# Delta rule products in turn between column halves, both directions in step, and the HGRN output's attention product with all 128 rows

## The chip, the cores and the metric

One core of one Trainium2 chip runs the whole program. The metric is the device time of one execution in microseconds. The engines are PE (matmuls), DVE (vector), ACT (activations), POOL and SP; SP issues most of the transfers.

## What is computed

One layer of a trunk over 2048 latent and 256 context tokens, width 1024. Four token mixers (HGRN2, gated DeltaNet, Fourier, Mamba-2 SSD) are merged by sigmoid gates, and a mixture of experts follows. Two of the mixers matter here. Both work on 4 heads of 64 channels, in chunks of 64 tokens, in a forward and a backward direction whose outputs are added:

```python
# gated DeltaNet, one direction: t_mat = I + strictly lower (beta k k^T L); u, w solve t_mat
def step(S, inp):
    u_c, w_c, qk_c, qd_c, kd_c, gl_c = inp
    v_new = u_c - w_c @ S
    o_c = qd_c @ S + qk_c @ v_new
    S = jnp.exp(gl_c)[..., None, None] * S + jnp.einsum("bhjd,bhje->bhde", kd_c, v_new)
    return S, o_c
# HGRN2, one direction
o = att @ vc + (qc * jnp.exp(g)) @ S
```

The gates are `sigmoid(h @ w_gate[g] + b_gate[g])`, four projections of 1024 x 1024 for all latent tokens.

## The kernel before

The program is written with a tile framework. The methods are called one after the other (`front`): projections, masks and decays, `gdn_heads` and `gdn_invert` (delta rule: matrices per head, inverses of 32x32 blocks), then `gdn_merge`, `gdn_chain`, `hgrn`, `ssd`, `fourier` and `gates`. When the kernel is built, the framework lays the instructions of each engine in one fixed order, with the order of the program text as priority and durations that it estimates, and adds the semaphores. So instructions of `gates` (its matmuls are lines 114 to 116 with the tiles `whi`, `wlo`, `h2h`, `h3h` and so on), though last in the text, stand between those of the mixers on PE wherever the planner saw room.

- `gdn_merge` (L1164 on) runs six rounds: two pairs of heads `b` times three groups of six token blocks. A round loads the inverted blocks D, R, F, B, and `pairs` (L1198) makes 64x64 products of them on PE (L1206): `Ao` with D, the result with R (it fills the open quarter of F and B), then the decayed keys `K` with F and with B (the W products). `i` is the head in the pair, `a` the half of the 128-token block. Each call of `pairs` makes four groups of six products; the group lies in one row half and one column half of the array, and ACT empties its PSUM tile (64 partitions). D and R use row half `a` and column half `a`; the W products use row half `a` and column half 64 to 127. F, B and W go to DRAM as `gLW`.
- `gdn_chain` (L1235 on) runs 36 steps over the chunks for each direction `d`. The tile `gX` holds 64 rows of values U and 64 rows of state S, for four heads. A step loads `gLt` (from `gLW`), makes four products of it with `gX` (L1266, K = 128 rows, output in partitions 0 to 63), multiplies by beta on DVE (L1267), decays S (L1273), makes four products of the keys `gKt` (64 rows) with U (L1278, output in partitions 64 to 127), adds them to S on DVE (L1279), and, for latent chunks, makes the output with `gAt` (L1287), whose four products write the lower and the upper 64 partitions in turn. The two directions follow each other within a step, each with its own PSUM tiles.
- `hgrn` (L826 on) works head by head. At its end each of 32 chunks gets two products that are summed in PSUM: L926, attention times values, takes 64 rows (`o` is the chunk's half of the tiles `hatt` and `hv`), and L928, state times queries, takes 128 rows. `hv` has zeros in the other half of the rows: they are written once, since L906 uses the tile with all rows. The output partitions are the half `r` that belongs to the head.

Of the kernel before, what the change touches and what calls it, by code (L numbers as in the profile page):

```python
# [18 lines left out]
D = 1024  # L19
# [26 lines left out]
class Kernel:  # L46
# [773 lines left out]
    def hgrn(self, p):  # L820
# [17 lines left out]
        for h in range(H):  # L838
# [80 lines left out]
            for g in range(2):  # L919
                for a in range(2):  # L920
                    ps = self.two()
                    o = 64 * a
# [100 lines left out]
    def gdn_heads(self, p):  # L1023
# [16 lines left out]
        for b in range(2):  # L1040
            for g in range(0, self.NP, G):
# [59 lines left out]
                for d, mk in ((0, "ge"), (1, "le")):  # L1101
                    ro = (d * nl + l0 // 64) * 32768
                    T = tl("gA", 4)
                    nc.vector.tensor_mul(T[:, ml:], Z[:, ml:], bc(self.tm[mk])[:, ml:])
                    for a in range(2):
                        nc.sync.dma_start(ap(rec, ro + a * 32768 + 128 * b, [[256, 64], [65536, nq], [1, 128]]),
                                          T[64 * a:64 * a + 64, ml:].rearrange("p m h i -> p m (h i)"))

                    gq = p.tile([128, n], F32, name="gE", bufs=2)
                    for i in range(2):  # L1110
                        r = slice(64 * i, 64 * i + 64)
                        self.bc_time(gq[:, 128 * ml:], 8 + 4 * d + 2 * b + i, CTX + l0, 128 * nq, r, 64)
                    nc.vector.tensor_mul(gq[:, 128 * ml:], gq[:, 128 * ml:], qT[:, 128 * ml:])
                    for i in range(2):
                        r = slice(64 * i, 64 * i + 64)
                        nc.sync.dma_start(ap(rec, ro + 64 * 256 + 64 * (2 * b + i), [[256, 64], [32768, 2 * nq], [1, 64]]),
                                          gq[r, 128 * ml:].rearrange("p (c i) -> p c i", i=64))
# [50 lines left out]
    def gdn_merge(self, p):  # L1168
# [10 lines left out]
        for b in range(2):  # L1179
            for g in range(0, NP, G):  # L1180
# [27 lines left out]

                def ev_q(ps, c, a, i):
                    nc.scalar.activation(Q[c, :, i], ps[c], AF.Copy)  # L1210
                pairs(Ao, blk["D"], ev_q)

                def ev_x(ps, c, a, i):
                    r0 = slice(64 * a, 64 * a + 32)
                    r1 = slice(64 * a + 32, 64 * a + 64)
                    nc.scalar.activation(blk["F"][r0, :, i, 32:], ps[r0, :, 32:], AF.Copy, scale=-1.0)
                    nc.scalar.activation(blk["B"][r1, :, i, :32], ps[r1, :, :32], AF.Copy, scale=-1.0)
                pairs(Q, blk["R"], ev_x)
                for d, n in ((0, "F"), (1, "B")):
                    K = p.tile(B4, F32, name="gK4", bufs=1)  # L1220
# [3 lines left out]
                    Wt = p.tile([128, G, 2, 2, 64], F32, name="gW4", bufs=1)  # L1224

                    def ev_w(ps, c, a, i):
                        nc.scalar.activation(Wt[c, :, a, i], ps[c], AF.Copy, scale=-1.0)
                    pairs(K, blk[n], ev_w, 64)
                    ro = (d * 36 + 2 * g) * 32768 + 128 * b
                    for a in range(2):  # L1230
                        nc.sync.dma_start(ap(gL, ro + a * 32768, [[256, 64], [65536, G], [1, 128]]),
                                          blk[n][64 * a:64 * a + 64].rearrange("p m h i -> p m (h i)"))
                    nc.sync.dma_start(ap(gL, ro + 64 * 256, [[256, 64], [32768, 2 * G], [1, 128]]),
                                      Wt[64:].rearrange("p m a h i -> p (m a) (h i)"))

    def gdn_chain(self, p, fp):
        nc = self.nc
        nl, ncx = SEQ // 64, CTX // 64
        gL, rec = self.dram("gLW", (2, 36, 128, 256)), self.dram("gAT", (2, nl, 128, 256))
        kh, gV = self.dram("gKH", (2, 36, 64, 256)), self.dram("gV", (TOT, W))  # L1240
        bU = p.tile([64, self.NT, 2, 8], F32, name="gbU")
        for a in range(2):
            nc.vector.tensor_copy(bU[:, :, a], self.beta[64 * a:64 * a + 64])
        oG = p.tile([128, 2, SEQ], F32, name="goT")
        order = [list(range(36)), list(range(ncx))[::-1] + list(range(ncx, 36))[::-1]]

        def newX(d, c):
            x = p.tile([128, 4, 64], F32, name=f"gX{d}", bufs=3)
            nc.sync.dma_start(x[:64], ap(gV, c * 64 * W, [[W, 64], [64, 4], [1, 64]]))
            return x  # L1250
        X = []
        for d in range(2):
            x = newX(d, order[d][0])
            nc.vector.memset(x[64:], 0.0)
            X.append(x)
        seen = set()
        for s in range(36):
            for d in range(2):
                c = order[d][s]
                x = X[d]  # L1260
                last = s == 35
                lw = p.tile([128, 4, 64], F32, name=f"gLt{d}", bufs=2)
                nc.sync.dma_start(lw, ap(gL, (d * 36 + c) * 32768, [[256, 128], [64, 4], [1, 64]]))
                ps = self.mx()
                for h in range(H):
                    nc.tensor.matmul(ps[:64, h * 64:h * 64 + 64], lw[:, h], x[:, h], start=True, stop=True)  # L1266
                nc.vector.tensor_tensor(x[:64], ps[:64, :256].rearrange("p (h e) -> p h e", e=64),  # L1267
                                        bU[:, c // 2, c % 2, 4 * d:4 * d + 4][:, :, None].to_broadcast([64, 4, 64]), op=OP.mult)
                if not last:
                    kt = p.tile([64, 4, 64], F32, name=f"gKt{d}", bufs=2)  # L1270
                    nc.sync.dma_start(kt, ap(kh, (d * 36 + c) * 16384, [[256, 64], [64, 4], [1, 64]]))
                    xn = newX(d, order[d][s + 1])
                    nc.vector.tensor_tensor(xn[64:], x[64:],  # L1273
                                            self.gl64[64:, c % 2, c // 2, 4 * d:4 * d + 4][:, :, None].to_broadcast([64, 4, 64]),
                                            op=OP.mult)
                    ps = self.mx()
                    for h in range(H):
                        nc.tensor.matmul(ps[64:, h * 64:h * 64 + 64], kt[:, h], x[:64, h], start=True, stop=True)  # L1278
                    nc.vector.tensor_tensor(xn[64:], xn[64:], ps[64:, :256].rearrange("p (h e) -> p h e", e=64), op=OP.add)  # L1279
                    X[d] = xn  # L1280
                if c >= ncx:
                    n = c - ncx
                    at = p.tile([128, 4, 64], F32, name=f"gAt{d}", bufs=2)
                    nc.sync.dma_start(at, ap(rec, (d * nl + n) * 32768, [[256, 128], [64, 4], [1, 64]]))
                    ps = self.mx()
                    for h in range(H):
                        nc.tensor.matmul(ps[64 * (h % 2):64 * (h % 2) + 64, h // 2 * 64:h // 2 * 64 + 64], x[:, h],  # L1287
                                         at[:, h], start=True, stop=True)
                    o = oG[:, :, n * 64:n * 64 + 64]
                    pv = ps[:, :128].rearrange("p (b i) -> p b i", i=64)  # L1290
# [964 lines left out]
```

## Time and profile before

| what | value |
|---|---|
| median of 3 runs | 3985.44 us (3971.31 to 3986.7) |
| the profiled execution | 3978.21 us, its span 3976.4 us |
| mean granted TensorE clock | 0.937 of 2.4 GHz |
| busy: PE, DVE, ACT, POOL | 3668.2, 2457.5, 1277.1, 904.1 us |

The span runs from the first to the last instruction. [...] Busy time of PE counts modelled ends of pipelined matmuls.

### The profile page before, as it was taken

The page shows a single profiled execution, that of the slowest core. Times are in us where ns is not written, and L with a number is a line of the kernel's source. Part 1 is how long each engine was busy: PE and PEld are TensorE (multiplying, and loading weights), DVE is VectorE, ACT ScalarE, POOL GpSimd, SP SyncE. Part 2 cuts the span into 40 slices and gives each one's busy share as a digit, 9 for nine tenths or more (in the row PEclk, how much of TensorE's full clock was granted, in tenths as well). Part 3 has the DMA queues.
Part 4 walks back from the last instruction along what each step waited for, and adds up shares of the span by engine and source line. Part 5 has one row for each costly group of instructions (what it writes and reads, how often), then busy time and mean ns, then how long its engine had stood idle before and what let it go on. Part 6 is the DMA issues. An engine that isn't in the chain of part 4 may idle for free. (4 is left out here: it accounts for less than half of the span.)

```text
span 3976.4 us, 60130 instructions
## 1 busy us (share of the span) xinstructions
PE 3668.2 (92%) x23407; PEld 3052.9 (77%) x23407; DVE 2457.5 (62%) x4454; ACT 1277.1 (32%) x1950; POOL 904.1 (23%) x636
## 2 busy tenths in 40 slices
PE   6999999998899999899889989994899999999997
PEld 3887778787777676667767767773799999999886
DVE  7538752275626477373875577788565555555887
ACT  3422232122425122142224322212334444444443
POOL 2000013311212110122341246564010000101243
PEclk9999999998969899897899999996899999999998
DMA  7534448756435456423356766643475665766875
GB/s 244 191 112 137 125 112 197 185 136 156 121 88 129 137 155 196 135 81 100 94 145 207 233 215 189 199 143 136 146 221 182 216 223 193 226 208 208 284 264 182
DMA packets 596812, 680.93 MB, mean 171 GB/s; under 512 B 152656, under 2 KB 469552, under 8 KB 593328
## 3 DMA queue, kind: packets, MB, share of 16 engines
q1 hardware_dynamic: 537136, 537.08, 44.2%
q0 software_dynamic: 24800, 90.71, 8.4%
q10 hardware_dynamic: 34592, 49.29, 3.6%
q8 instruction: 185, 3.03, 0.3%
q14 instruction: 99, 0.81, 0.1%
HBM read 514.88 MB, written 162.06 MB: 170 GB/s over the span
## 5 line engine op out<-in xcount | busy, mean ns | idle before, releaser
L107 POOL TENSOR_TENSOR wlo<-wraw,whi 128x1024 fp32r<-128x1024 f32 x60 | 147.5, 2458 | 687.9 <-ACT whi L105 622.8
L114 PE MATMUL big<-h2h,whi 128*128 128x512 f32 x704 | 295.3, 419 | 3.9 <-ACT ev L1566 3.9
L114 PE MATMUL mx<-exh,wgateh 128*128 128x256 f32 x1024 | 296.0, 289 | 0.0
L116 PE MATMUL big<-h2h,wlo 128*128 128x512 f32 x704 | 295.5, 420 | 0.5 <-DVE wlo L107 0.5
L115 PE MATMUL big<-h2l,whi 128*128 128x512 f32 x704 | 295.2, 419 | 0.0
L115 PE MATMUL mx<-exl,wgateh 128*128 128x256 f32 x1024 | 290.7, 284 | 0.0
L116 PE MATMUL mx<-exh,wgatel 128*128 128x256 f32 x1024 | 290.5, 284 | 0.0
L116 PE MATMUL big<-h3h,wlo 128*128 128x512 f32 x704 | 290.2, 412 | 0.0
L114 PE MATMUL big<-h3h,whi 128*128 128x512 f32 x704 | 289.9, 412 | 0.0
L115 PE MATMUL big<-h3l,whi 128*128 128x512 f32 x704 | 289.9, 412 | 0.0
L115 PE MATMUL mx<-exl,wuph 128*128 128x256 f32 x1024 | 289.8, 283 | 0.0
L116 PE MATMUL mx<-exh,wupl 128*128 128x256 f32 x1024 | 289.8, 283 | 0.0
L114 PE MATMUL mx<-exh,wuph 128*128 128x256 f32 x1024 | 289.8, 283 | 0.0
L2077 POOL DMA_INDIRECT d_acc<-ey,ix x30 | 50.7, 1690 | 780.2 <-DVE ey L2070 741.1
L116 PE MATMUL big<-wdh,hidl 128*128 128x512 f32 x496 | 196.4, 396 | 10.9 <-DVE hidl L107 10.9
L107 DVE TENSOR_TENSOR wdl<-wdr,wdh 128x1024 fp32r<-128x1024 f32 x124 | 153.7, 1240 | 81.5 <-ACT wdh L105 81.4
L115 PEld LDWEIGHTS mx<-exl,wgateh 128*128 128x128 f32 x1024 | 197.3, 193 | 2.8 <-DVE exl L107 0.3
L114 PEld LDWEIGHTS mx<-exh,wgateh 128*128 128x128 f32 x1024 | 197.3, 193 | 2.5
L107 DVE TENSOR_TENSOR wgatel<-wgr,wgateh 128x2048 fp32r<-128x2048 f32 x62 | 151.0, 2436 | 76.2 <-ACT wgateh L105 76.1
L2031 ACT ACTIVATE sg<-mx 128x256 f32<-128x256 f32 x128 | 49.1, 383 | 462.5 <-PE mx L116 462.5
L2032 DVE TENSOR_TENSOR sg<-sg,mx 128x256 f32<-128x256 f32 x128 | 53.7, 420 | 231.9 <-ACT sg L2031 231.8
L116 PEld LDWEIGHTS mx<-exh,wgatel 128*128 128x128 f32 x1024 | 196.8, 192 | 0.0
(641 smaller groups left out, 9875.3 us busy)
## 6 DMA issues: line engine op xcount, KB each, us to landing
wgr<-in_w_ff_gate_dram SPq DMA_DIRECT2D x64, 1024.0 KB
wgr<-in_w_ff_up_dram SPq DMA_DIRECT2D x64, 1024.0 KB
wdr<-in_w_ff_down_dram SPq DMA_DIRECT2D x128, 512.0 KB
wraw<-in_w_gate_dram POOLq DMA_DIRECT2D x64, 512.0 KB, 5.0
d_th<-ev ACTq DMA_DIRECT2D x128, 256.0 KB
bt<-d_th SPq DMA_DIRECT2D x128, 256.0 KB
adr<-in_ada_w_dram SPq DMA_DIRECT2D x128, 128.0 KB
bw<-in_w_branch_dram SPq DMA_DIRECT2D x64, 256.0 KB
```

The lines of the kernel that those rows point to most:

```text
L107: return (eng or self.nc.vector).tensor_tensor(lo, src, hi, op=OP.subtract)
L114: self.nc.tensor.matmul(ps, wh, xh, start=first and k == 0, stop=False)
L115: self.nc.tensor.matmul(ps, wh, xl, start=False, stop=False)
L116: self.at_pe = self.nc.tensor.matmul(ps, wl, xh, start=False, stop=last and k == n - 1).ins
L2031: silu.append(nc.scalar.activation(sg, ps[:, :CAP], AF.Silu).ins)
L2032: self.at_dve = nc.vector.tensor_mul(sg, sg, ps[:, CAP:]).ins
L2077: nc.gpsimd.indirect_dma_start(out=acc, out_offset=bass.IndirectOffsetOnAxis(ap=ix[e][:, k:k + 1], axis=0), in_=weighted(e, k), in_offset= ...
```

## The change

- HGRN output: L926 takes all 128 rows of `hv` and `hatt` in place of 64.
- Merge: in a group the products of the two halves `a` (D and R) or of the two directions (W) follow each other in turn, with one PSUM tile of 128 partitions for both; ACT empties 128 partitions at once. The keys of both directions are made first, in two tiles (`gK40`, `gK41`).
- Chain: direction 0 keeps U in partitions 0 to 63 and S in 64 to 127, direction 1 has them swapped. In a step the products of both directions stand in one group, head by head, direction by direction, in one PSUM tile; the DVE work follows for one direction and then the other. The output products come after both.
- The addresses of the blocks stored for direction 1 (`gLW`, `gAT`) are swapped to fit.

```diff
-    nc.tensor.matmul(out, v[o:o + 64, CTX // 128 + c // 2, a], att[o:o + 64, c // 2, :],
-                     start=True, stop=False)
+    nc.tensor.matmul(out, v[:, CTX // 128 + c // 2, a], att[:, c // 2, :], start=True, stop=False)
...
-    def pairs(lhs, rhs, evac, col=None):
-        for i in range(2):
-            for a in range(2):
-                ps = self.mx()
-                r = slice(64 * a, 64 * a + 64)
-                c = r if col is None else slice(col, col + 64)
-                for m in range(G):
-                    nc.tensor.matmul(ps[c, m * 64:m * 64 + 64], lhs[r, m, i], rhs[r, m, i], start=True, stop=True)
-                evac(ps[:, :64 * G].rearrange("p (m i) -> p m i", i=64), c, a, i)
+    def pairs(i, lhs, rhs):
+        ps = self.mx()
+        for m in range(G):
+            for a in range(2):
+                r = slice(64 * a, 64 * a + 64)
+                nc.tensor.matmul(ps[r, m * 64:m * 64 + 64], lhs[r, m, i], rhs[r, m, i], start=True, stop=True)
+        return ps[:, :64 * G].rearrange("p (m i) -> p m i", i=64)
+    for i in range(2):
+        nc.scalar.activation(Q[:, :, i], pairs(i, Ao, blk["D"]), AF.Copy)
...
+    rows = [slice(64, 128), slice(0, 64)]
+    for i in range(2):
+        for a in range(2):
+            r = slice(64 * a, 64 * a + 64)
+            ps = self.mx()
+            for m in range(G):
+                for d, n in ((0, "F"), (1, "B")):
+                    nc.tensor.matmul(ps[rows[d], m * 64:m * 64 + 64], Ks[d][r, m, i], blk[n][r, m, i],
+                                     start=True, stop=True)
+            nc.scalar.activation(Wt[:, :, a, i], ps[:, :64 * G].rearrange("p (m i) -> p m i", i=64), AF.Copy,
+                                 scale=-1.0)
...
+    U, S = [slice(0, 64), slice(64, 128)], [slice(64, 128), slice(0, 64)]
...
+    for s in range(36):
+        cs = [order[d][s] for d in range(2)]
...
+        ps = self.mx()
+        for h in range(H):
+            for d in range(2):
+                nc.tensor.matmul(ps[U[d], h * 64:h * 64 + 64], lw[d][:, h], X[d][:, h], start=True, stop=True)
+        for d, c in enumerate(cs):
+            nc.vector.tensor_tensor(X[d][U[d]], rows4(ps[U[d], :256]),
+                                    bU[U[d], c // 2, c % 2][:, :, None].to_broadcast([64, 4, 64]), op=OP.mult)
...
+            kt = p.tile([128, 4, 64], F32, name="gKt", bufs=2)
+            for d, c in enumerate(cs):
+                nc.sync.dma_start(kt[U[d]], ap(kh, (d * 36 + c) * 16384, [[256, 64], [64, 4], [1, 64]]))
+                X[d] = newX(d, order[d][s + 1])
...
+            ps = self.mx()
+            for h in range(H):
+                for d in range(2):
+                    nc.tensor.matmul(ps[S[d], h * 64:h * 64 + 64], kt[U[d], h], old[d][U[d], h], start=True, stop=True)
+            for d in range(2):
+                nc.vector.tensor_tensor(X[d][S[d]], X[d][S[d]], rows4(ps[S[d], :256]), op=OP.add)
```

## Rows read from the trace of the kernel before

**Rows 1.** Busy time in four stretches: stretch, length, busy (instructions), granted clock, DMA
```profile
980.00:1290.00 310.00, 291.29 (x2711) 228.29 (x2712) 161.85 (x401) 132.53 (x284) 67.58 (x56) 0.86 0.45 111
1290.00:1550.00 260.00, 256.87 (x2479) 184.15 (x2479) 165.24 (x435) 47.81 (x107) 23.57 (x22) 0.93 0.52 155
1550.00:1875.00 325.00, 294.20 (x1837) 224.28 (x1834) 161.36 (x439) 94.31 (x170) 57.88 (x45) 0.86 0.36 113
1875.00:2265.00 390.00, 346.49 (x1716) 278.93 (x1715) 265.97 (x439) 125.30 (x210) 127.66 (x97) 0.93 0.54 167
```

**Rows 2.** Groups by line on PE: tile shape, count, busy, mean ns, idle before
```profile
L926 PE MATMUL two<-hatt,hv 64*64 64x64 f32 x256 | 57.7, 324 | 6.6 <-ACT hoT L929 6.6
L928 PE MATMUL two<-hQ,hS 128*64 128x64 f32 x256 | 57.5, 329 | 7.4 <-DVE hS L914 7.4
L1266 PE MATMUL mx<-gX,gLt 128*64 128x64 f32 x576 | 49.4, 230 | 0.0
L1278 PE MATMUL mx<-gX,gKt 64*64 64x64 f32 x560 | 48.5, 228 | 1.7 <-DVE gX L1267 1.5 <-ACT hqz L886 0.2
L1287 PE MATMUL mx<-gAt,gX 128*64 128x64 f32 x512 | 29.9, 238 | 0.0
```

**Rows 3.** Busy time of PE for L1206 alone, in one stretch
```profile
940.00:1300.00 360.00, 83.93 (x1152) 0.86 0.49 122
```

**Rows 4.** Timeline of PE near the first head's output: start, duration, instruction, count
```profile
1119.94 0.91 PE L1206 MATMUL mx<-g4B,gK 64*64 64x64 f32 x12
1120.78 0.50 PE L115 MATMUL big<-h3l,whi 128*128 128x512 f32 x1
...
1141.85 0.47 PE L926 MATMUL two<-hatt,hv 64*64 64x64 f32 x2
1142.25 0.47 PE L928 MATMUL two<-hQ,hS 128*64 128x64 f32 x2
...
1143.87 0.69 PE L928 MATMUL two<-hQ,hS 128*64 128x64 f32 x4
1144.48 0.47 PE L926 MATMUL two<-hatt,hv 64*64 64x64 f32 x2
```

**Rows 5.** Timeline of PE in the chain: eight passes in one half
```profile
1389.41 0.67 PE L1278 MATMUL mx<-gX,gKt 64*64 64x64 f32 x8
1390.01 0.50 PE L116 MATMUL big<-h3h,wlo 128*128 128x512 f32 x1
```

**Rows 6.** Timeline of PE: passes in turn between column halves, two places
```profile
1719.35 0.69 PE L864 MATMUL two<-hqz,hk 128*64 128x64 f32 x16 [1.57 <-DVE hk L892]
1719.97 0.50 PE L116 MATMUL big<-h2h,wlo 128*128 128x512 f32 x1
...
765.28 1.44 PE L1081 MATMUL mx<-gk 64*64 64x64 f32 x48 [0.49 <-DVE gZ L1100]
766.65 0.50 PE L114 MATMUL big<-h1h,whi 128*128 128x512 f32 x1
```

**Rows 7.** Timeline of PE in the merge: first and last row of a D and R run
```profile
1264.94 2.29 PE L1206 MATMUL mx<-g4D,gAo 64*64 64x64 f32 x45
...
1269.53 0.49 PE L906 MATMUL two<-hv,hkT 128*128 128x128 f32 x2
```

**Rows 8.** Busy time in and behind the first head's output (columns as in rows 1)
```profile
1140.00:1165.00 25.00, 25.00 (x135) 18.11 (x136) 0.00 (x0) 2.89 (x6) 3.24 (x3) 0.50 0.10 24
1165.00:1184.00 19.00, 19.00 (x145) 15.41 (x145) 0.00 (x0) 6.97 (x17) 3.09 (x4) 0.50 0.21 44
```

**Rows 9.** Groups by line on DVE, 1290 to 1550 us
```profile
L1267 DVE TENSOR_TENSOR gX<-mx,gbU 64x256 f32<-64x256 f32 x72 | 30.0, 417 | 22.2 <-PE mx L1266 20.4 <-PE two L864 0.4 <-DMA gKt<-d_gKH 0.2
```

**Rows 10.** Timeline of all engines at the chain's start
```profile
1291.39 0.58 SPq L1263 DMA_DIRECT2D gLt<-d_gLW  x1
...
1294.67 0.54 PEld L1266 LDWEIGHTS mx<-gX,gLt 128*64 128x64 f32 x8 [0.37 <-DMA gLt<-d_gLW]
```

**Rows 11.** Busy time of PE for matmuls that read wlo (L116 of the gates)
```profile
1290.00:1550.00 260.00, 46.20 (x101) 0.93 0.52 155
```

More of the change, by code (lines that the diff above doesn't have):

```diff
@@ L921, in hgrn @@
                     ps = self.two()
-                    o = 64 * a
                     for j in range(8):
@@ L1197, in gdn_merge @@
                 Q = p.tile(B4, F32, name="gQ4", bufs=1)
-                def pairs(lhs, rhs, evac, col=None):
-                    for i in range(2):
+                def pairs(i, lhs, rhs):
+                    ps = self.mx()
+                    for m in range(G):
                         for a in range(2):
-                            ps = self.mx()
                             r = slice(64 * a, 64 * a + 64)
-                            c = r if col is None else slice(col, col + 64)
-                            for m in range(G):
-                                nc.tensor.matmul(ps[c, m * 64:m * 64 + 64], lhs[r, m, i], rhs[r, m, i], start=True, stop=True)
-                            evac(ps[:, :64 * G].rearrange("p (m i) -> p m i", i=64), c, a, i)
[L1209 to L1220, printed above, removed]
+                            nc.tensor.matmul(ps[r, m * 64:m * 64 + 64], lhs[r, m, i], rhs[r, m, i], start=True, stop=True)
[3 more added lines that the diff above has]
+                for i in range(2):
+                    ps = pairs(i, Q, blk["R"])
+                    for a in range(2):
+                        r0 = slice(64 * a, 64 * a + 32)
+                        r1 = slice(64 * a + 32, 64 * a + 64)
+                        nc.scalar.activation(blk["F"][r0, :, i, 32:], ps[r0, :, 32:], AF.Copy, scale=-1.0)
+                        nc.scalar.activation(blk["B"][r1, :, i, :32], ps[r1, :, :32], AF.Copy, scale=-1.0)
+                Ks = []
+                for d in range(2):
+                    K = p.tile(B4, F32, name=f"gK4{d}", bufs=1)
                     c = 4 * d + 2 * b
@@ L1223, in gdn_merge @@
                                             op=OP.mult)
[L1224 to L1228, printed above, removed]
+                    Ks.append(K)
+                Wt = p.tile([128, G, 2, 2, 64], F32, name="gW4", bufs=1)
+                rows = [slice(64, 128), slice(0, 64)]
+                for i in range(2):
+                    for a in range(2):
[7 more added lines that the diff above has]
+                                             scale=-1.0)
+                for d, n in ((0, "F"), (1, "B")):
                     ro = (d * 36 + 2 * g) * 32768 + 128 * b
                     for a in range(2):
-                        nc.sync.dma_start(ap(gL, ro + a * 32768, [[256, 64], [65536, G], [1, 128]]),
+                        nc.sync.dma_start(ap(gL, ro + a * 32768 + 64 * d * 256, [[256, 64], [65536, G], [1, 128]]),
                                           blk[n][64 * a:64 * a + 64].rearrange("p m h i -> p m (h i)"))
-                    nc.sync.dma_start(ap(gL, ro + 64 * 256, [[256, 64], [32768, 2 * G], [1, 128]]),
-                                      Wt[64:].rearrange("p m a h i -> p (m a) (h i)"))
+                    nc.sync.dma_start(ap(gL, ro + 64 * (1 - d) * 256, [[256, 64], [32768, 2 * G], [1, 128]]),
+                                      Wt[rows[d]].rearrange("p m a h i -> p (m a) (h i)"))
     def gdn_chain(self, p, fp):
@@ L1240, in gdn_chain @@
         kh, gV = self.dram("gKH", (2, 36, 64, 256)), self.dram("gV", (TOT, W))
-        bU = p.tile([64, self.NT, 2, 8], F32, name="gbU")
+        U, S = [slice(0, 64), slice(64, 128)], [slice(64, 128), slice(0, 64)]
+        bU = p.tile([128, self.NT, 2, 4], F32, name="gbU")
         for a in range(2):
-            nc.vector.tensor_copy(bU[:, :, a], self.beta[64 * a:64 * a + 64])
+            for d in range(2):
+                nc.vector.tensor_copy(bU[U[d], :, a], self.beta[64 * a:64 * a + 64, :, 4 * d:4 * d + 4])
         oG = p.tile([128, 2, SEQ], F32, name="goT")
@@ L1248, in newX, with rows4 @@
             x = p.tile([128, 4, 64], F32, name=f"gX{d}", bufs=3)
-            nc.sync.dma_start(x[:64], ap(gV, c * 64 * W, [[W, 64], [64, 4], [1, 64]]))
+            nc.sync.dma_start(x[U[d]], ap(gV, c * 64 * W, [[W, 64], [64, 4], [1, 64]]))
             return x
+        def rows4(ps):
+            return ps.rearrange("p (h e) -> p h e", e=64)
         X = []
@@ L1253, in gdn_chain @@
             x = newX(d, order[d][0])
-            nc.vector.memset(x[64:], 0.0)
+            nc.vector.memset(x[S[d]], 0.0)
             X.append(x)
@@ L1257, in gdn_chain @@
         for s in range(36):
[L1258 to L1263, printed above, removed]
+            cs = [order[d][s] for d in range(2)]
+            last = s == 35
+            lw = []
+            for d, c in enumerate(cs):
+                lw.append(p.tile([128, 4, 64], F32, name=f"gLt{d}", bufs=2))
+                nc.sync.dma_start(lw[d], ap(gL, (d * 36 + c) * 32768, [[256, 128], [64, 4], [1, 64]]))
@@ new lines, in gdn_chain @@
+            ps = self.mx()
[5 more added lines that the diff above has]
+                                        bU[U[d], c // 2, c % 2][:, :, None].to_broadcast([64, 4, 64]), op=OP.mult)
+            old = list(X)
+            if not last:
+                kt = p.tile([128, 4, 64], F32, name="gKt", bufs=2)
+                for d, c in enumerate(cs):
+                    nc.sync.dma_start(kt[U[d]], ap(kh, (d * 36 + c) * 16384, [[256, 64], [64, 4], [1, 64]]))
+                    X[d] = newX(d, order[d][s + 1])
+                    nc.vector.tensor_tensor(X[d][S[d]], old[d][S[d]],
+                                            self.gl64[S[d], c % 2, c // 2, 4 * d:4 * d + 4][:, :, None].to_broadcast([64, 4, 64]),
+                                            op=OP.mult)
@@ L1264, in gdn_chain @@
                 ps = self.mx()
                 for h in range(H):
[L1266 to L1280, printed above, removed]
@@ L1281, in gdn_chain @@
+                    for d in range(2):
+                        nc.tensor.matmul(ps[S[d], h * 64:h * 64 + 64], kt[U[d], h], old[d][U[d], h], start=True, stop=True)
+                for d in range(2):
+                    nc.vector.tensor_tensor(X[d][S[d]], X[d][S[d]], rows4(ps[S[d], :256]), op=OP.add)
+            for d, c in enumerate(cs):
                 if c >= ncx:
```

6 lines of the change are left out of this document (3 added, 3 removed).

## Prediction

> **What bounds the kernel now.** I read the table of stages first. From 980 to 2265 us the token mixers run (merge of the delta rule's blocks, its chain, the HGRN heads, then SSD and Fourier), and the gate projections, which no mixer needs, are laid between their instructions. PE is busy for 291.3 of 310 us, 256.9 of 260, 294.2 of 325 and 346.5 of 390, together 1188.9 of 1285 (92.5%); DVE for 754.5 (59%) [rows 1]. So PE ends last in this stretch, in the chain's stage almost without a gap. Of what lies ahead, the change alters store addresses only, and of SSD, Fourier and all behind them nothing: what it saves must be saved here, and the later stages then start earlier as they are.
>
> Next, the list of groups by line: the lines to be changed cost PE 57.7 + 57.5 us (HGRN output, L926 and L928), 49.4 + 48.5 us (chain, L1266 and L1278) [rows 2] and 83.9 us (merge, L1206) [rows 3]. Each fp32 product stands there as two passes (the 72 chain groups of four products are x576). L1287 is the row to look at: products of the same shape as L1266, and a mean busy share of 29.9 / 512 = 0.058 us a pass against 49.4 / 576 = 0.086 us. The difference in the code is that L1287 writes the lower and the upper column half in turn, L1266 only the lower.
>
> Then the timeline of PE, read from start to start, because ends are modelled and overlap. Eight passes in one column half: 1389.41 to 1390.01, 0.60 us [rows 5]. Twelve: 1119.94 to 1120.78, 0.84 us [rows 4]. So 0.06 us for each pass more, and some 0.12 us once for the neighbour of another shape. In turn between halves: sixteen 128x64 passes of L864 take 1719.35 to 1719.97, 0.62 us, and 48 passes of L1081, with 64 rows, 765.28 to 766.65, 1.37 us, 0.0285 us each [rows 6]. Sixteen in turn cost what eight in one half cost. In the HGRN output the two products of a chunk have different shapes (64x64 and 128x64) and follow each other in turn: at the 1.2 GHz level one product lasts 1141.85 to 1142.25, 0.40 us, while a stretch of two L928 products in a row takes 1143.87 to 1144.48, 0.61 us, so the second of equal shape costs only 0.21 us [rows 4].
>
> **The change part by part.**
>
> *HGRN output.* 256 products (512 passes) stay, all become 128x64 in one column half. At 2.4 GHz a product then takes 2 x 0.06 = 0.12 us, 31 us in all; at 1.2 GHz 0.21 us, 54 us. Now they cost 115.2 us [rows 2]. In head 0 the clock stands at 0.50 from 1140 to 1165 us, while these products run, and in the 19 us behind them [rows 8]; I take heads 1 to 3 as alike. Whether denser products keep it up no row shows, so I take the slow price: 61 us saved, 84 as the upper bound; the lower bound is 0, if not the shape but the accumulating pair costs. I take 61 because the one place with equal neighbours stands in this very stretch. The other operand rows are zeros that the kernel writes today (half of each hv tile), and the same semaphores are waited for, so nothing is added.
>
> *Chain.* Per step two groups of 8 in one half become one group of 16 in turn, for L1266 and for L1278: 36 x 0.62 us where 72 x 0.60 stood. Half of 49.4 + 48.5 goes [rows 2]: 49 us. L1266 has its exact row in L864. L1278 afterwards changes row half and column half together, into one bank; no row has that, so 24 us of the 49 are open: bounds 25 and 49, and I take 49, since the nearest row, the merge's D and R runs, crosses from one diagonal quadrant to the other every 12 passes and does 96 passes (3 records each of D and R stand elsewhere in the listing) in 4.59 us, 0.048 each, less than the 0.06 within a group [rows 7] (there the bank changes too).
>
> *What joining the directions costs.* DVE, ACT and DMA work is equal in number. But both directions now wait for each other twice a step. On the path of a step stand 0.62 + 2 x 0.42 + 0.62 + 2 x 0.42 = 2.9 us and four hand-overs (DVE from L1267, 0.417 us; the adds behind L1278 are as long) [rows 9]; a step has 260 / 36 = 7.2 us now [rows 1]. The cover is gate work: its L116 matmuls alone take 46.2 us in this stage, with L114 and L115 about three times that, 3.9 us a step [rows 11], and the HGRN heads. Without it the chain would show 2 x 0.84 us of DVE per step, 60 us. Behind a waiting L1278 on PE stand only these gate products and L1287. I cost it at nothing, and by a discount below.
>
> *Merge.* Six rounds. The W products: 8 groups of 12 (0.84 us) become 4 of 24, each 0.62 + 8 x 0.0285 = 0.85 us: 6.7 to 3.4 us. D and R: 96 passes, 4.59 us now, at 0.0285 us 2.7 us. Together 11.3 to 6.1, 46% off, so 39 us of the 83.9. If the diagonal pairs gain nothing, 6 x 3.3 = 20. I take 39. ACT empties half as many, fuller tiles; POOL's K products are as many, but both directions' now come before the first W product, and the F half is stored with the B half rather than before it; PE has gates and HGRN work to do while they wait, and if that cover fails a round loses at most the F group's 3.4 us.
>
> The swapped halves of the stored blocks change DMA addresses only; the chain's loads are as many and as large.
>
> [...] Sixteen L864 passes with all 128 rows, in turn between column halves, take 0.62 us, eight in one half 0.60 [rows 5, 6]. [...]
>
> **The sum.** 61 + 49 + 39 = 149 us of PE. Not all of it moves the end, since PE would now wait more often for DVE and DMA. In the HGRN output DVE is idle and PE full (0.00 and 25.00 of 25 us [rows 8]), so I count 85%: 52 us. In the chain PE is at 99%, DVE at 64% [rows 1]: 75%, for the joining: 37 us. In the merge PE has 6% of gaps and the rounds wait for loads: 60%, 23 us. These shares are my choice; they give 112 us. From the profiled execution, 3978.2 us (span 3976.4 and 1.8 around it): 3866 us. The median of the runs, 3985.4, stands 7 us higher; I forecast 3865, which lies 3% under either.
>
> **Rivals.**
> 1. *The clock stays up.* If the denser HGRN products hold 2.4 GHz, 23 us more go there, and some of the half-speed stretches behind them (19 us in head 0) shrink by half: 3830 us. For: the chain, small products mixed with gates, holds 0.93 [rows 1]. Against: in head 0 it is down for all but the first of these products [rows 8]. 0.12.
> 2. *The gain turns into idle PE.* The merge rounds and heads may be set by loads and by DVE; at 35% of 149: 3926 us. For: PE already has 96 us of gaps in the stretch. Against: from 1140 to 1165 us DVE has no work at all [rows 8]. 0.14.
> 3. *Only row halves overlap.* Then L1266 and W gain nothing (25 and 20 us less): 52 + 0.75 x 24 + 0.6 x 19 = 81, so 3897 us. Against: L864 and L1081 [rows 6]. 0.01. [...]
> 4. *Diagonal quadrants don't overlap in one bank.* L1278, D and R gain nothing: 52 + 0.75 x 25 + 0.6 x 20 = 83, so 3895 us. Only the missing row speaks for it. [...] 0.07.
> 5. *The new order undoes it.* The order on each engine is worked out anew at build; if the gates are laid where nothing waits, gaps eat the 112 us: within 0.5%, 3975 us. 0.05.
> 6. *Slower: the joined step waits for its loads.* A step needs eight loads, on SP's queue, one behind the other; one issue takes 0.58 us and the first products started 3.3 us after theirs [rows 10]. If every step showed issues, landing and its own path, 8 x 0.58 + 3.3 + 2.9 = 10.8 us against 7.2, the chain would lose 130 us and HGRN and merge would save 75: 4033 us. It decides from 7.2 + (75 + 20) / 36 = 9.8 us a step on. Against: the loads are issued a step or two ahead into two and three buffers. 0.05.
>
> **Numbers.** 0.56 for the forecast, the rest as given. A difference of 0.5% (20 us) is about what a measurement of this kernel can tell from none. Faster: 0.56 + 0.12 + 0.14 + 0.07 + 0.01 = 0.90; same 0.05; slower 0.05. The range takes in rivals 1 to 4: below, all 149 us and 84 instead of 61 for HGRN would be 3806; above, rival 2 with some waiting at the joins, 3935. So 3800 to 3935.
>
> **What would show it.** L928 and L926 both 128x64, their sum near 54 us (31 if the clock stays up); L1266 and L1278 near 25 us each in groups of 16; L1206 near 45; the chain's stage down from 260 to about 220 us; PE's wait at the second product still a few us; SSD to the end as long as before. I am wrong if L1278's passes stay at 0.06 us or more, if PE's idle time before L1278 grows beyond 1 us a step, or if the stages shorten and the end of the gates (2265 us) does not move.

## The result and the profile after

The changed kernel takes 3845.24 us (median of 4 runs, 3843.23 to 3848.93) against 3983.44 for the kernel before (4 runs on the same chip, 3971.31 to 3986.7): ratio 0.9659, 95% interval 0.9637 to 0.9682, or 138 us less. The profiled execution took 3848.93 us with a span of 3847.1, which is 129.3 us under the span of before. PE runs as many matmuls as before (23407), ACT 36 instructions fewer; PE's busy time fell from 3668.2 to 3523.6 us, that of DVE, ACT and POOL changed by at most 20.

The stages after. The columns are those of [rows 1]: stretch, length, busy time (and instructions) of PE, of its weight loads, of DVE, ACT and POOL, then granted clock, busy share of the DMA engines and GB/s. The borders stand near the merge's start, the chain's start and end, the end of the HGRN heads with what follows them, and the end of the gates:

```profile
940.00:1215.00 275.00, 232.17 (x2656) 184.27 (x2656) 167.62 (x405) 112.22 (x238) 76.25 (x75) 0.94 0.62 145
1215.00:1434.00 219.00, 214.66 (x2477) 147.51 (x2476) 164.49 (x434) 47.22 (x105) 27.08 (x24) 0.98 0.62 182
1434.00:1740.00 306.00, 274.06 (x1975) 216.31 (x1973) 184.03 (x488) 101.55 (x188) 61.42 (x49) 0.92 0.41 125
1740.00:2137.00 397.00, 355.03 (x1746) 284.68 (x1745) 263.39 (x435) 126.11 (x209) 125.86 (x95) 0.93 0.53 163
```

The chain's stage lasts 219 us where it lasted 260. The merge's last product starts at 1203 us (1285 before), the chain's last output product at 1433 (1549), the last HGRN product at 1698 (1832), the last gate tile is written at 2132 (2260). So of the 128 us that the gates end earlier, 6 were there at the merge's start (956 us against 962), the merge's stage gave 76, the chain's 34, the remaining heads 18, and 6 were lost in SSD and Fourier. From there to the end both kernels take 1715 to 1716 us. But a stage's gain is not all due to the lines that it is named after, for the HGRN heads' outputs are spread over the stages. From its first to its last product the merge's stage takes 322 us before and 247 after; in the run with the HGRN edit alone (hgrn_only, below) it takes 299, in the run with all but that edit (without_hgrn) 271. So 24 us of its gain belong to head 0's output and 51 to the merge itself. The chain's stage goes from 264 to 241 us by the HGRN edit alone (head 1's output lies in it) and to 246 without it: 23 and 18 us.

The whole stretch from 900 us to the last gate tile, first before, then after:

```profile
900.00:2260.00 1360.00, 1255.34 (x9017) 968.57 (x9015) 796.78 (x1798) 416.19 (x784) 292.27 (x245) 0.90 0.48 139
```

```profile
900.00:2132.00 1232.00, 1111.21 (x8998) 861.20 (x8996) 800.41 (x1792) 397.66 (x748) 291.48 (x244) 0.94 0.54 153
```

PE lost 144 us of work, its gaps grew from 105 to 121 us, and 128 us are left. In both traces the granted clock stands at 1.00 or at 0.50, and a value between them is a mean over a stretch; so a mean c over a length means a share of 2(1 - c) at 0.50: about 270 us before, about 150 after.

The groups by line that answer to [rows 2]:

```profile
L925 PE MATMUL two<-hatt,hv 128*64 128x64 f32 x256 | 37.7, 248 | 6.8 <-ACT hoT L927 6.8
L926 PE MATMUL two<-hQ,hS 128*64 128x64 f32 x256 | 37.1, 248 | 13.1 <-DVE hS L914 13.1
L1280 PE MATMUL mx<-gX,gLt 128*64 128x64 f32 x576 | 35.7, 232 | 1.3 <-DMA d_th<-ev 1.3
L1296 PE MATMUL mx<-gX,gKt 64*64 64x64 f32 x560 | 35.0, 227 | 0.2 <-DVE gX L1282 0.2
L1306 PE MATMUL mx<-gAt,gX 128*64 128x64 f32 x512 | 29.5, 235 | 1.5 <-DMA gAt<-d_gAT 1.5
```

The HGRN output's two lines went from 115.2 to 74.8 us, the chain's two from 97.9 to 70.7 (not to 49). L1306 is untouched and costs the same. PE hardly waits before the second product (0.2 us).

The merge, as in [rows 3] but as two lines (D and R at L1203, W at L1230), and the timeline of a D run behind head 0's output:

```profile
940.00:1215.00 275.00, 23.25 (x576) 21.42 (x576) 0.94 0.62 145
940.00:1215.00 275.00, 19.76 (x576) 17.72 (x576) 0.94 0.62 145
```

```profile
1115.84 1.61 PE L1203 MATMUL mx<-g4D,gAo 64*64 64x64 f32 x48
1117.34 1.58 PE L1203 MATMUL mx<-g4R,gQ 64*64 64x64 f32 x46
```

Together 43.0 us against 83.9. The 48 passes that go from one diagonal quadrant to the other, in one bank, take 1.50 us, 0.031 us each: close to the 0.0285 of a turn between column halves alone [rows 6].

The chain near its middle, start to start:

```profile
1294.95 0.33 PE L1296 MATMUL mx<-gX,gKt 64*64 64x64 f32 x2
1295.20 0.50 PE L116 MATMUL big<-h3h,wlo 128*128 128x512 f32 x1
1295.54 0.40 PE L114 MATMUL big<-h3h,whi 128*128 128x512 f32 x1
1295.87 0.68 PE L1296 MATMUL mx<-gX,gKt 64*64 64x64 f32 x14
1296.47 0.50 PE L115 MATMUL big<-h3l,whi 128*128 128x512 f32 x1
```

The group of 16 is cut: 2 passes, two gate matmuls, then 14. So it is in all 35 steps of L1296 and in 31 of the 36 of L1280. The first product (2 passes) needs only the forward direction's DVE result, so the order computed at build can let it go first and fill the wait for the other with gates; chain_rev below tests this reading. The two parts cost 0.25 + 0.60 us; [rows 5] had 0.60 for 8.

Head 3's output in both kernels. Before (timeline, then the granted clock in two stretches of it):

```profile
1806.93 0.32 PE L926 MATMUL two<-hatt,hv 64*64 64x64 f32 x2
1807.18 0.33 PE L928 MATMUL two<-hQ,hS 128*64 128x64 f32 x2
...
1809.10 0.47 PE L926 MATMUL two<-hatt,hv 64*64 64x64 f32 x2
```

```profile
1806.00:1809.00 3.00, 2.33 (x20) 1.79 (x20) 0.85 (x3) 0.00 (x0) 0.00 (x0) 1.00 0.00 0
1810.00:1831.00 21.00, 21.00 (x98) 14.43 (x98) 0.00 (x0) 2.40 (x4) 0.00 (x0) 0.50 0.00 1
```

After, the same:

```profile
1688.49 0.42 PE L926 MATMUL two<-hQ,hS 128*64 128x64 f32 x2
1688.70 0.42 PE L925 MATMUL two<-hatt,hv 128*64 128x64 f32 x2
...
1694.09 0.28 PE L926 MATMUL two<-hQ,hS 128*64 128x64 f32 x2
1694.21 0.28 PE L925 MATMUL two<-hatt,hv 128*64 128x64 f32 x2
```

```profile
1687.00:1692.00 5.00, 5.00 (x49) 5.00 (x49) 0.00 (x0) 0.49 (x1) 0.00 (x0) 0.50 0.01 3
1693.00:1698.00 5.00, 5.00 (x68) 4.29 (x67) 0.00 (x0) 1.73 (x3) 0.00 (x0) 1.00 0.00 0
```

In both kernels PE waits some 2.9 us for DVE just before these products. Before, they start at full clock, 0.255 us each; 2.4 us behind the wait the clock falls, and it stays at 0.50 for the rest of the head, 0.40 us each, though PE shows no gap (21.00 of 21 us). After, the clock falls within the wait, so they start at 0.21 us each, and it comes back while they run: 0.12 us each.

From head 3 alone the fall could be due to the wait. Head 1 decides that. In without_hgrn, whose products alternate as before, PE's last wait ahead of them is 0.21 us, more than 5 us before the clock falls (at 1336.7 us, 3.3 us into the products); it comes back only at 1371, behind the last of them:

```profile
1334.00:1336.00 2.00, 2.00 (x18) 1.46 (x19) 1.75 (x6) 0.00 (x0) 0.00 (x0) 1.00 0.47 131
1336.00:1338.00 2.00, 2.00 (x20) 1.51 (x19) 0.00 (x0) 0.28 (x1) 0.00 (x0) 0.68 0.12 32
1348.00:1350.00 2.00, 2.00 (x11) 1.42 (x12) 0.00 (x0) 0.00 (x0) 0.00 (x0) 0.50 0.00 0
```

In the changed kernel, with the same short wait ahead, head 1's output runs at full clock from end to end (1309.6 to 1321 us):

```profile
1310.00:1312.00 2.00, 2.00 (x36) 1.85 (x34) 1.88 (x6) 0.43 (x2) 0.00 (x0) 1.00 0.61 187
1318.00:1320.00 2.00, 2.00 (x36) 1.70 (x35) 0.99 (x3) 0.01 (x1) 0.44 (x1) 1.00 0.38 100
```

So the alternating products bring the clock down here without a wait, and where a wait did it they keep it down (head 3 before: at 0.50 from 1809 us to behind the head's last product). In the kernel before, head 1's output is also all that lowers the clock of the chain's stage to the 0.93 of [rows 1]: 37.6 us at 0.50, from 1344.8 on.

### The profile page after: what moved, and what is told of

Read it like the earlier page. It is cut to its first block, busy times and chain, and to the rows that moved or that the text cites. A ratio compares the mean times of both kernels' runs of the same rounds, so it can differ in the third digit from the quotient of the medians.

```text
span 3847.1 us, 60078 instructions
## 1 busy us (share of the span) xinstructions
PE 3523.6 (92%) x23407; PEld 2944.0 (77%) x23407; DVE 2463.3 (64%) x4456; ACT 1257.6 (33%) x1914; POOL 904.1 (23%) x636
## 4 chain that ended last, share of the span: by engine, by line
PE 59%; DVE 17%; DMA 9%; issue 8%; ACT 3%; POOL 3%; SPq 1%; POOLq 0%; ACTq 0%; DVEq 0%
PE big L116 12%; PE big L114 12%; PE big L115 11%; PE mx L115 4%; PE mx L114 4%; PE mx L116 4%; DVE hS L914 1%; PE two L864 1%; DMA bt<-d_th 1%; DVE hk L892 1%; DVE hQ L890 1%; DVE iX L1153 1%; DVE iT L1151 1%; PE mx L1782 1%; DVE sS L1409 1%
## 5 line engine op out<-in xcount | busy, mean ns | idle before, releaser
L116 PE MATMUL big<-h2h,wlo 128*128 128x512 f32 x704 | 292.7, 416 | 2.1 <-POOL wlo L107 2.1
L116 PE MATMUL mx<-exh,wgatel 128*128 128x256 f32 x1024 | 290.4, 284 | 0.0
L116 PE MATMUL mx<-exh,wupl 128*128 128x256 f32 x1024 | 290.0, 283 | 0.0
L116 PE MATMUL big<-h3h,wlo 128*128 128x512 f32 x704 | 287.2, 408 | 0.0
L116 PE MATMUL big<-wdh,hidl 128*128 128x512 f32 x496 | 195.6, 394 | 12.9 <-DVE hidl L107 12.8
L114 PEld LDWEIGHTS mx<-exh,wuph 128*128 128x128 f32 x1024 | 196.7, 192 | 0.0
```

What stands on the lines that cost most here:

```text
L114: self.nc.tensor.matmul(ps, wh, xh, start=first and k == 0, stop=False)
L116: self.at_pe = self.nc.tensor.matmul(ps, wl, xh, start=False, stop=last and k == n - 1).ins
```

## The experiments

Ten other kernels ran beside the changed one, and the changed one once more on another chip (after_again). Each ratio is to the kernel before on the same chip; "lines" are busy times in us of the groups of HGRN output and chain; the clock is that of the stretch from 900 us to the last gate tile.

| run | median us | ratio, 95% interval | HGRN lines | chain lines | clock |
|---|---|---|---|---|---|
| before | 3983.44 | 1 | 115.2 | 97.9 | 0.90 |
| changed | 3845.24 | 0.9659 (0.9637 to 0.9682) | 74.8 | 70.7 | 0.94 |
| hgrn_only | 3899.77 | 0.9790 (0.9764 to 0.9817) | 68.8 | 95.2 | 0.94 |
| without_hgrn | 3917.81 | 0.9842 (0.9815 to 0.9868) | 111.1 | 72.2 | 0.90 |
| hgrn_turned | 3884.31 | 0.9758 (0.9732 to 0.9784) | 70.9 | 71.3 | 0.92 |
| hgrn_64both | 3838.45 | 0.9634 (0.9615 to 0.9654) | 71.7 | 70.6 | 0.94 |
| merge_old | 3898.71 | 0.9785 (0.9766 to 0.9803) | 77.4 | 70.5 | 0.94 |
| chain_old | 3882.65 | 0.9736 (0.9702 to 0.9769) | 77.7 | 95.8 | 0.93 |
| chain_blocks | 3867.9 | 0.9711 (0.9690 to 0.9732) | 67.0 | 83.0 | 0.94 |
| chain_rev | 3836.27 | 0.9632 (0.9611 to 0.9654) | 67.2 | 49.5 | 0.93 |
| both_turns | 3824.02 | 0.9592 (0.9565 to 0.9618) | 43.1 | 49.8 | 0.93 |
| hgrn_halves | 3866.36 | 0.9705 (0.9678 to 0.9732) | 39.1 | 72.9 | 0.92 |
| after_again | 3856.4 | 0.9680 (0.9652 to 0.9708) | 69.2 | 72.3 | 0.92 |

**The HGRN edit alone.** On the kernel before, the change's first hunk and nothing else:

```
-                        nc.tensor.matmul(out, v[o:o + 64, CTX // 128 + c // 2, a], att[o:o + 64, c // 2, :],
+                        nc.tensor.matmul(out, v[:, CTX // 128 + c // 2, a], att[:, c // 2, :],
                                          start=True, stop=False)
```

> The kernel before with one edit: the HGRN output's first product takes all 128 rows. Theory (what costs is the change between a 64-row and a 128-row matmul at every product, whatever the rest of the kernel does): its two lines fall from 115 us to about 75, the half-speed stretch of head 0's output (44 us in the kernel before) shrinks to under 20, and the time falls by 50 to 70 us, to about 3920. Rival (the clock came back because of the merge's and the chain's new order): the stretch at half speed stays, the lines cost 55 to 60 us at that clock, and the time falls by 40 us or less, to 3945 or more.

85 us, more than the theory's 50 to 70; the lines fell to 68.8 us. Within head 0's output PE waits 3.5 us for DVE, as it did before (3.4), and the clock falls behind the wait, as it did before; but now it is down for 3.4 us and not for 44, for it comes back while the products run:

```profile
1140.00:1145.00 5.00, 5.00 (x68) 5.00 (x67) 0.00 (x0) 1.18 (x2) 0.00 (x0) 0.74 0.00 0
1145.00:1150.00 5.00, 5.00 (x92) 4.69 (x91) 0.00 (x0) 2.90 (x6) 3.17 (x3) 1.00 0.42 94
```

The rival falls: this one line brings the clock of the stretch from 0.90 to 0.94 with merge and chain as they were.

**All but the HGRN edit.** The same two lines the other way round, in the changed kernel.

> The changed kernel with the HGRN output's first product back at 64 rows: what is left is the merge and the chain. If the parts add up, this run and the one with the HGRN edit alone together save the 138 us of the whole: 65 to 90 us here, 3895 to 3918. If the parts need each other for the clock, this one saves less than 60 us (over 3925) and the two sums do not reach 138 us.

3918 us, 67 below before, at the edge of what adding up allowed. 85 + 67 = 152 us, against the whole's 138: the parts don't need each other. Whether they share something the runs don't tell, since the three intervals are each some 10 us wide to either side. The clock stays at 0.90, as before. Its products, in head 3:

```profile
1748.52 0.47 PE L926 MATMUL two<-hatt,hv 64*64 64x64 f32 x2
1748.92 0.47 PE L928 MATMUL two<-hQ,hS 128*64 128x64 f32 x2
1749.33 0.47 PE L926 MATMUL two<-hatt,hv 64*64 64x64 f32 x2
```

**Half as many changes of shape.** In that kernel, odd chunks take the two products in the other order:

```
-                        nc.tensor.matmul(out, v[o:o + 64, ...], att[o:o + 64, c // 2, :], start=True, stop=False)
-                        nc.tensor.matmul(out, S[:, 3 + c, :], Q[:, c * 64:c * 64 + 64], start=False, stop=True)
+                        for t in ((0, 1) if j % 2 == 0 else (1, 0)):
...
```

> As the run without the HGRN edit (64 rows), but every second output chunk takes its two products in the other order, so that two 64-row and two 128-row products follow each other and there are half as many changes of the shape; the number of matmuls, of rows and of columns is the same. Theory (each change of shape costs): the two lines' sum falls about half of the way from 115 to 75 us, to 90 to 100, and the time by 15 to 35 us from the run without the edit. Rival (a 64-row product is slow by itself, or each accumulating pair is): the sum stays at 110 to 115 us and the time within 8 us of that run.

```profile
1716.49 0.69 PE L931 MATMUL two<-hatt,hv 64*64 64x64 f32 x4
1717.11 0.69 PE L928 MATMUL two<-hQ,hS 128*64 128x64 f32 x4
1717.73 0.69 PE L931 MATMUL two<-hatt,hv 64*64 64x64 f32 x4
```

The three rows of without_hgrn above and these are all at clock 0.50. Two passes and a change of shape take 0.403 us, four passes and a change 0.617: so two passes take 0.214 us and a change 0.19. The 0.214 is the price after the change (1688.49 to 1688.70 in the changed kernel's head 3), for 64-row and 128-row passes alike. At full clock, 0.255 - 0.117 = 0.14 us a change. The time fell by 33.5 us, about half of the 73 between without_hgrn and the changed kernel. The clock stands in the middle too, but 0.92 for the stretch is what after_again shows as well, without any change of shape; over the whole span it was 0.939 to 0.943 in the four executions of without_hgrn, 0.944 to 0.949 in the four here, and 0.949 to 0.956 in the nine of the changed kernel. Head 1's output runs at full clock here, head 3's still at half. The busy sum fell further than expected only because modelled ends of equal neighbours overlap; start to start is the measure. Counted so, the output's products take 93 us in without_hgrn, 61 here, 38 in the next run and 40 in the changed kernel.

**No change of shape, half the rows.** Both products at 64 rows; the kernel leaves out half of the sum of the product with the states, so it serves for its time alone:

```
-                        nc.tensor.matmul(out, S[:, 3 + c, :], Q[:, c * 64:c * 64 + 64], start=False, stop=True)
+                        nc.tensor.matmul(out, S[o:o + 64, 3 + c, :], Q[o:o + 64, c * 64:c * 64 + 64], start=False, stop=True)
```

> The changed kernel with both products of the HGRN output at 64 rows (the product with the states too: half of its sum is left out). No change of shape at all, half of the rows idle; the waits are the same. Theory (it is the change of shape that costs, and that keeps the clock down): the passes follow each other as fast as 128-row ones (0.107 us at 1.2 GHz, 0.058 at 2.4), the time at half clock before the gates end is as in the changed kernel (about 150 us, not 250), and the time is within 10 us of 3845. Rival (64-row products fill too little of the array for the clock): passes as fast, but 190 us or more at half clock, and 3865 or more.

```profile
1676.17 0.28 PE L926 MATMUL two<-hatt,hv 64*64 64x64 f32 x2
1676.28 0.28 PE L928 MATMUL two<-hQ,hS 64*64 64x64 f32 x2
1676.40 0.28 PE L926 MATMUL two<-hatt,hv 64*64 64x64 f32 x2
```

3838 us, the clock at 0.94, 0.117 us a product. Filling all 128 rows is not what helps here; equal neighbours are. With these four runs both the price of the output and the clock follow the number of changes of shape, not the number of rows. Whether a change acts on the clock by itself, or by spreading the passes over more time, no run tells apart.

**The chain's cut undone.** In both products of the changed kernel:

```
-                for d in range(2):
+                for d in (1, 0):
```

> The changed kernel with the two directions taken in the opposite turn in the chain's two products (backward first), so that a group's first product needs the later of the two VectorE results and nothing of the group can be issued ahead of it. Theory (the chain's products gained 27 us and not 49 because each group of 16 passes was cut into 2 and 14 with gate matmuls between): the two lines fall from 70.7 us to about 50 and the time by 10 to 20 us from the changed kernel, to 3825 to 3835. Rival (the cut costs nothing, or the joined group waits for the second direction and PE is idle there): the lines' idle time rises by as much as their busy time falls, and the time stays within 6 us of 3845 or rises.

```profile
L1280 PE MATMUL mx<-gX,gLt 128*64 128x64 f32 x576 | 25.2, 228 | 6.0 <-issue 3.4 <-DMA gLt<-d_gLW 2.7
L1296 PE MATMUL mx<-gX,gKt 64*64 64x64 f32 x560 | 24.3, 227 | 4.0 <-issue 2.4 <-DMA gKt<-d_gKH 0.9 <-DVE hk L892 0.7
```

```profile
1338.68 0.69 PE L1280 MATMUL mx<-gX,gLt 128*64 128x64 f32 x16
1339.30 0.50 PE L115 MATMUL big<-h2l,whi 128*128 128x512 f32 x1
```

Sixteen passes in 0.62 us, and the two lines at 49.5 us: the prediction's 49, to the microsecond. Of the 21 us that they lose, the time gives 9 by the medians and 11 by the ratios, at the lower edge of what the theory foretold; the two kernels ran on different chips and the intervals of the ratios overlap, so these two runs alone don't show a gain in time. PE's idle time before the two lines grew from 1.5 to 10.0 us, now behind loads and issue. So the theory holds for the passes, and the rival took over a third of what they gain.

**The chain in turn, and joined.** chain_old takes one direction after the other, with the changed kernel's row halves; chain_blocks keeps the joined step and swaps the two loops:

```
-            for h in range(H):
-                for d in range(2):
+            for d in range(2):
+                for h in range(H):
```

> The changed kernel with the chain's directions one after the other again (8 passes of one column half, the next direction later), on the changed kernel's row halves. Theory (the chain gained 27 us of passes and no more): its two lines go from 71 to 98 us and the time to 3862 to 3872. Rival (joining the steps had lengthened the waits of each step, so that undoing it gives some back): within 8 us of 3845.

> The changed kernel with the chain's directions joined in a step but not in turn: 8 passes of direction 0, then 8 of direction 1, in each product. Theory (what gains is the turn between column halves inside a group, not the joining): the lines stay near 98 us, as with the old chain, and the time within 8 us of that run. Rival (the joining gains, by fewer waits): the time within 8 us of 3845.

Undoing the chain's part costs 0.0077 of the time, 31 us (37 by the medians, on another chip); its lines go back to 95.8. The theory foretold the lines, but at most 27 us; the stretch's clock is lower too (0.93), and what makes the rest of the difference is open. chain_blocks fits neither of its expectations: its second product stays at 47.2 us, in separate groups of 8, but the first falls to 35.8 without any turn:

```profile
1308.96 0.97 PE L1280 MATMUL mx<-gX,gLt 128*64 128x64 f32 x16
1309.85 0.51 PE L115 MATMUL big<-h2l,whi 128*128 128x512 f32 x1
```

There the two blocks of 8 stand side by side, and 16 passes take 0.89 us where two groups alone take 1.20. Not having gate matmuls between them is worth something by itself, besides the turn. That 0.89 is also less than 0.12 + 16 x 0.06 was not resolved further.

**The merge's old order.** On the changed kernel's stored halves:

```
-                for i in range(2):
-                    nc.scalar.activation(Q[:, :, i], pairs(i, Ao, blk["D"]), AF.Copy)
...
+                pairs(Ao, blk["D"], ev_q)
...
+                    pairs(K, blk[n], ev_w, 64 * (1 - d))
```

> The changed kernel with the merge's products in the old order (12 passes of one quadrant at a time, forward and backward W apart), only its stored row halves as in the changed kernel. Theory (the merge gained its own 26 us of passes, 61 against 87, at 0.75 to 1): 3865 to 3872. Rival A (the merge stage's gain was the clock of head 0's output, which the HGRN edit alone gives): within 8 us of 3845. Rival B (the diagonal turn is what brings the clock up for the stage): 3885 or more.

50 us by the ratios, more than its lines' 35 (77.8 us here against 43.0; the 26 of the theory adds up four groups of which two run in turn and so overlap). Its executions spread: the profiled one took 3877.36 us at a mean clock of 0.954 over its span, the four others 3898 to 3905 at 0.946 to 0.948. So the median lies where rival B had it, and the theory's range is missed; only the profiled execution, with 0.94 in the stretch as in the changed kernel, comes near it (3877 against 3872). That the diagonal turn holds the clock up is therefore not shown: the one trace has it up without the turn, and why the clock differs between executions of one kernel was not tried.

**Further on the same road.** In hgrn_halves the HGRN output's even chunks go to the lower column half and the odd ones to the upper, in turn, in one PSUM tile; both_turns adds chain_rev's edit.

```
+                for j in range(8):
+                    for t in range(2):
+                        for a in range(2):
+                            out = ps[64 * a:64 * a + 64, j * 64:j * 64 + 64]
...
```

> Two further edits on the changed kernel: the chain's opposite turn (as in the run of that alone, 3836), and the HGRN output written so that even chunks go to the lower column half and odd chunks to the upper one, in turn, one PSUM tile for both. Theory (passes that alternate between column halves take 0.03 us in place of 0.058 at 2.4 GHz, accumulating pairs too): the HGRN output's 512 passes lose 14 us at full speed and up to 27 at half, the two lines' sum goes from 67 to under 45 us, and the time to 3812 to 3826. Rival (an accumulating pair can't overlap with its neighbour, or the two evictions of half the rows hold the next tile back): the passes stay at 0.058 us or the PSUM waits take the gain, and the time is within 6 us of 3836.

> The changed kernel with only the HGRN output's turn between column halves; the chain as in the changed kernel. Theory: 10 to 20 us under the changed kernel, 3825 to 3835, the same step as between the opposite turn alone and both together. Rival: within 6 us of the changed kernel.

> The changed kernel as it is, on the chip of the two runs above: 3840 to 3850.

The lines fall to 39 and 43 us, so accumulating pairs overlap in turn too. Alone this moves nothing, and the 10 to 20 us expected did not come: 0.9705 against 0.9680 for the changed kernel on the same chip; PE's busy time is 14 us lower (3528.1 against 3542.4) and its idle time 18 us higher (330.4 against 312.2). after_again also came out 11 us above the first runs of the same kernel, at a clock of 0.92 in the stretch rather than 0.94; by so much a comparison across chips may be wrong. With chain_rev's edit the kernel takes 3824 us, 0.9592, the best of all: 32 us below after_again on the same chip, with the ratios' intervals apart. Against hgrn_halves, also on this chip, it is 42 us (0.9705 to 0.9592, intervals apart): that is chain_rev's edit alone, and it shows a gain that the comparison across chips above could not. Its chain lines give 23 us of it; PE's other work falls by 17, with the clock of the stretch at 0.93 against 0.92.

## Why the prediction came out as it did

The forecast was 3865 us, 20 above the 3845 measured, with the time inside the range. The mechanisms of the passes were right, the clock was left out of the sum, and that the total lies so near is in part luck: the chain was forecast too high, the shares that reach the end too low, and the HGRN term is right by two errors that cancel.

- **HGRN output: 61 us forecast, about 58 measured, and the clock is in it.** The 115.2 us counted modelled ends; start to start, with the mean pass of 324 ns between 222 (full clock) and 368 (half), 70% of 256 products cost 0.403 us and the rest 0.255: 92 us. After, with 248 ns, 18% cost 0.213 and the rest 0.117: 34 us. So the prediction's 115 was some 20 us too high and its 54 as well: the slow price was the wrong choice, and that the difference came out near 61 is luck. I had read head 0's half clock as a state in which the products happened to run; the runs show that the changes of shape keep it there (44 us before, 3.4 in hgrn_only), and in head 1 bring it (34 us at 0.50 in without_hgrn, none in the changed kernel). What the prediction calls 2.4 and 1.2 GHz is the granted clock of 1.00 and 0.50: the traces show that share and no frequency. From start to start a 128x512 gate matmul takes 0.23 us at 1.00 (before, near 1188 us) and 0.43 us at 0.50 (near 1182 us).
- **Rival 1 (the clock stays up)** is therefore half true. With products of equal shape the clock comes back while they run (at 1692.4 us in head 3 of the changed kernel), and the time lies between the forecast and that rival's 3830 us. By busy time the clock's part outside the changed lines is 18 us (below).
- **Chain: 49 forecast, 27 measured.** The step that failed is "two groups of 8 become one group of 16": at build nearly all were cut into 2 and 14, and pay for a neighbour of another shape twice. The prediction had that price (0.12 us a neighbour) and did not ask whether the group stays whole. chain_rev's 49.5 us shows the rest of the step right, L1278's open 24 us included. The foretold 220 us for the chain's stage came (219), but by luck: 23 us of that gain are head 1's output.
- **Merge: 39 forecast, 41 measured** (83.9 to 43.0), half-clock passes included.
- **Rivals 3 and 4** are out. In chain_rev L1266's successor keeps all 128 rows and 16 of its passes in turn take 0.62 us, against 0.60 for 8 in one half. The weight loads show the same in the changed kernel: in L1280's group of 14 at 1299.44 us, two loads of one pair start 7 ns apart and take some 138 ns each. Diagonal quadrants in one bank take 0.031 us a pass, against 0.0285 in [rows 6].
- **The sum.** 58 + 27 + 41 = 126 us of the 149. PE's busy time in the stretch fell by 144; the other 18 are matmuls of the gates that now run at full clock more often. (Counting each matmul in the traces only up to the next start on PE, the fall is 58 us for the HGRN output, 26 for the chain, 39 for the merge and 21 for lines 114 to 116.) The gaps grew by 16. So 128 of 144, 89%, reached the gates' end, where my shares averaged 75%. The passes were forecast too high (the chain), the shares too low, and the clock's 18 us was no term.
- **Rivals 2, 5 and 6.** PE's gaps took 16 us, not 65% of the gain; waits put down to DMA ahead of the chain's three products are 2.8 us in all. They come later: in chain_rev a third and more of the gain goes to waits, in hgrn_halves all of it. The end of the gates did move, and the rest lasts as long as before, as foretold.

Each part taken out alone costs 73 us (HGRN), 50 (merge) and 31 (chain) by the ratios, 154 together against 136. The difference is within what the intervals of these ratios allow, so that the parts overlap is not shown.

## What to carry to other kernels

Look in the timeline for matmuls of differing tile shape in strict turn, and price each change of shape beside the passes; make neighbours equal, even if rows are zeros (85 us in hgrn_only), or put equal ones side by side (33.5 us from without_hgrn to hgrn_turned). Try small products that write one half of the columns in turn with others that write the other half: here 16 passes took 0.62 us in turn (chain_rev), against 0.60 for 8 in one half [rows 5]; the lines of accumulating pairs went from 69.2 us of busy time (after_again) to 39.1 (hgrn_halves), and a pass on diagonal quadrants took 0.031 us. But see in the final order that a group stays whole, by letting its first product need what arrives last (70.7 to 49.5 us in chain_rev). When PE's passes shrink, look what the clock did: here the half-clock stretches without a gap in PE went with the pattern of the products.

## What was not expected of the hardware

A change between 64-row and 128-row products cost 0.14 us at clock 1.00 (0.255 before against 0.117 in hgrn_64both) and 0.19 at 0.50 (without_hgrn and hgrn_turned), so it shrank less than the passes did (0.117 and 0.213 a product of two). PE lost its clock while it was shown as busy without a gap: in head 1 of without_hgrn it fell to 0.50 while products of alternating shape ran, more than 5 us after a wait of 0.21 us, and stayed there for 34 us. Products with half the rows and no change of shape held the clock as well as full ones (0.94 over the stretch in hgrn_64both and in the changed kernel). And executions of one kernel differed by 21 to 27 us with their mean clock (merge_old: 3877 at 0.954, 3898 to 3905 at 0.946 to 0.948).
